# Prompt tokens in the order of their residue modulo 4, and 64 x 64 score blocks for the dilated heads of a decoder layer

## The chip, the cores and the metric

The kernel runs on one core of a Trainium2 chip. The metric is the device time of one execution in microseconds (us). Five engines take part: TensorE (PE: matmuls, and PEld: its weight loads), VectorE (DVE), ScalarE (ACT), GpSimd (POOL) and SyncE (SP, which here only issues transfers). ACT and POOL issue transfers too.

## What is computed

One layer of a hybrid decoder, for a prompt of 256 tokens and for 8 sample tokens with caches, which share all weights (D = 2048, all float32). Cut to what matters here:

```python
h = rmsnorm(x, g) * (1 + sc1) + sh1                     # modulation from c @ w_ada
q, k, v, u, ga, gb = split(h @ w_in, [1536, 3072, 4608, 5120, 7168])
for g, (window, dil) in enumerate(((128, 1), (512, 4), (2048, 16))):    # 4 heads each
    # a query reads itself and the tokens dil, 2*dil, ..., window behind it, ALiBi penalty -m_h*|t-s|
    outs[g], lses[g] = dilated_attn_prompt(q[g], k[g], v[g], dil, slopes[g])
    new_kv[g] = last min(window, T) rows of k and v
o = sum_g softmax_g(lses)[g] * outs[g]                  # 512 wide
p = pool_mixer(u)     # trailing means over 2, 4, 8, 16 tokens minus the token, 128 channels each
x = x + gt1 * ((sigmoid(ga) * (o @ w_up_attn) + sigmoid(gb) * (p @ w_up_pool)) @ w_out)
x = x + gt2 * (square(relu(h2 @ w_mlp_up)) @ w_mlp_down)
y = rmsnorm(x, g_fin)
```

Since the mixture of the three groups weighs by their softmax denominators, one softmax over all keys of the three groups gives o at once, and that is what the kernel does.

## The kernel before

Activations lie with channels on the 128 partitions and tokens along the row: 256 prompt tokens in their natural order, then the 8 sample tokens (N = 264 columns). A weight matrix streams through five `raw` tiles of 1 MB (`load`, issued by SP). ACT casts a half of such a tile to `whi` (L244), DVE takes the rest as `wlo` (L245), and PE multiplies each 128 x 128 block three times (`mm3`, L255 to L257), 264 columns each. One `whi`/`wlo` pair (three buffers) serves 24 matmuls. Beside this GEMM the modulation matrix w_ada is read as a filler (`ada_part`, L362: matmuls on 32 columns of the array each, four positions side by side, written `pa`).

The order of the instructions on each engine is made by the tile framework when the kernel is built. It interleaves the GEMM of the gates (w_in from column 5120 on), the filler and the prompt's pooling and attention, and places the waits; each engine then runs its queue strictly in that order. Transfers issued by SP and ACT take eight completion counters in turn (DMAHW0 to 7), those of POOL eight others (DMASW0 to 7). A transfer waits on its issuing queue until the one that last used its counter has landed, and what stands behind it in that queue waits with it.

The stage that the change touches:

- `pooling` (L612): four sums on DVE (L632, `up` to `a` to `b`), the means (L642 to L646) into `z`, then a matmul with w_pool (L649). The weights w_pool and the constants are loaded by POOL (L157, L606, L608), which then issues nine small stores of the sample's rows (L712). POOL clears the 16 columns ahead of the tokens (L615).
- `rows(pair, g)` (L653): for two heads of a group, PE transposes K and V (L661) into one of two PSUM buffers `px`, ACT copies them out (L666) and issues the stores to the new caches (L669). V stays, tokens on partitions, for the attention.
- `attend(slot)` (L672): for each half of the queries and the three heads of a slot, scores against all earlier keys (L679, 128 or 256 keys), the penalty and mask from `dist` (DVE, L681), one softmax (L684 to L687: a maximum on DVE, an exponential and a scaling on ACT), transposes of the weights (L692), and their product with V (L697).

The two pairs of heads follow each other: three calls of `rows`, then `attend` for two slots. The tokens of x come in at L403 and L404 and leave at L1089.

Of the kernel before, what the change touches and what calls it, by code (L numbers as in the profile page):

```python
# [30 lines left out]
T = 256  # L31
NS = 8
# [6 lines left out]
NEG = -1e30  # L39
# [16 lines left out]
def _consts():  # L56
    cols, at = [], 0

    def put(name, a):
        nonlocal at  # L60
        b = np.zeros((128, a.shape[1]), np.float32)
        b[:a.shape[0]] = a
        CONSTS[name] = (at, a.shape[1])
        cols.append(b)
        at += a.shape[1]
# [42 lines left out]
    r = i[:, None] % 32  # L108
    put("pick", np.concatenate([(r == hh * 8 + np.arange(8)[None, :]) * 1.0 for hh in range(4)], axis=1))
    marks.append(at)  # L110
    for g, dil in enumerate(DIL):
        t, s = i[:, None] + 128, np.arange(256)[None, :]
        d = t - s
        ok = (d >= 0) & (d % dil == 0) & (d <= 128 * dil)
        put(f"dist{g}", np.where(ok, -d, NEG))
    return np.concatenate(cols, axis=1).astype(np.float32), marks


# [4 lines left out]
def step_kernel(ctx, tc, x_prompt, x_sample, vectors, c_sample, kv0, kv1, kv2, state_pool, w_ada, w_in, w_up_attn,  # L123
# [472 lines left out]
    xpool.__exit__(None, None, None)  # L596
    ppool = tc.tile_pool(name="pp", bufs=1)
    ap = ppool.__enter__()
    dist = ap.tile([128, 3, 256], F32, name="dist")
    wp = ap.tile([128, 4, 128], F32, name="wpool")  # L600
    srow = ga_flat[:120, 416:928]
    mark = nc.gpsimd.tensor_copy(dummy, qkv[:, 0, 0:1])
    with tc.issue_after(mark.ins):
        nc.gpsimd.dma_start(srow, state_pool[0].rearrange("b j c -> (b j) c"))
        con_load(1, ap, nc.gpsimd)
        nc.gpsimd.dma_start(wp, w_pool.rearrange("g c d -> c g d"))  # L606
        a = CONSTS["dist0"][0]
        nc.gpsimd.dma_start(dist, consts[:, a:a + 768].rearrange("p (g c) -> p g c", g=3))  # L608


    def pooling():
        a = ga_flat[:, 2016:3104].rearrange("p (g t) -> p g t", g=4)  # L612
        b = ga_flat[:, 928:2016].rearrange("p (g t) -> p g t", g=4)
        for t in (up, a, b):
            nc.gpsimd.memset(t[:, :, :16], 0.0)  # L615
        us = up[:, :, 16 + T:]
        pr = px([15, 512])
        for g in range(4):
            nc.tensor.transpose(pr[:, g * 128:(g + 1) * 128], up[:, g, 16 + T - 15:16 + T], ident)
        prs = ap.tile([128, 768], F32, name="pt")[:15, :512]  # L620
# [5 lines left out]
        prs = ap.tile([128, 768], F32, name="sc")[:NS, :512]  # L626
        nc.scalar.copy(prs, pr)
        nc.gpsimd.dma_start(nps[0, :, 14], prs)
        src, dst = up, a
# [9 lines left out]
        nc.vector.tensor_add(z[:, :, T:], us, pw)  # L639
        for g, w in enumerate(WIN):  # L640
# [3 lines left out]
            nc.vector.scalar_tensor_tensor(z[:, g, 16:T], win[:, g, 32:], 1.0 / w, up[:, g, 32:16 + T], op0=OP.mult,  # L644
                                           op1=OP.subtract)
        nc.vector.tensor_sub(z[:, :, :16], t16, up[:, :, 16:32])  # L646
        for g in range(4):
            ps = px([128, N])
            nc.tensor.matmul(ps, wp[:, g], z[:, g], start=True, stop=True)  # L649
            nc.scalar.activation(z[:, g], ps, AF.Copy, scale=p_scale[:, g:g + 1])  # L650


    def rows(pair, g):  # L653
        hd = 4 * g + 2 * pair
        for kv in range(2):
            t0 = 1 if g == 0 and kv == 0 else 0
            src = qkv[:, 12 * (1 + kv) + hd:12 * (1 + kv) + hd + 2]
            p = px([128, 2, 256])
            for t in range(t0, 2):
                for j in range(2):  # L660
                    nc.tensor.transpose(p[:, j, t * 128:(t + 1) * 128], src[:, j, t * 128:(t + 1) * 128], ident)  # L661
            if kv:
                dst = src[:, :, :T]
            else:
                dst = ap.tile([128, 2, 256], F32, name="krow", bufs=3)
            nc.scalar.copy(dst[:, :, t0 * 128:], p[:, :, t0 * 128:])  # L666
            for t in range(1 if g == 0 else 0, 2):
                r0 = 0 if g == 0 else t * 128
                nc.scalar.dma_start(nkp[g][0, 0, r0:r0 + 128, kv, 2 * pair:2 * pair + 2, :],  # L669
                                    dst[:, :, t * 128:(t + 1) * 128])  # L670

    def attend(slot):  # L672
        for qt in range(2):
            nk = qt + 1
            sc = ap.tile([128, 3, 256], F32, name="sc")[:, :, :nk * 128]
            for g in range(3):
                hd = 4 * g + slot
                p = px([128, nk * 128])
                nc.tensor.matmul(p, qkv[:, hd, qt * 128:(qt + 1) * 128], qkv[:, 12 + hd, :nk * 128],  # L679
                                 start=True, stop=True)  # L680
                nc.vector.scalar_tensor_tensor(sc[:, g], dist[:, g, 256 - nk * 128:], SLOPES[hd], p,  # L681
                                               op0=OP.mult, op1=OP.add)
            m = ap.tile([128, 4], F32, name="m", bufs=2)
            nc.vector.tensor_reduce(m[:, 0:1], sc, axis=AX.XY, op=OP.max, negate=True)  # L684
# [3 lines left out]
            pt = ap.tile([128, 3, 2, 128], F32, name="pt")  # L688
            for kb in range(nk):
                p = px([128, 3, 128])  # L690
                for g in range(3):
                    nc.tensor.transpose(p[:, g], sc[:, g, kb * 128:(kb + 1) * 128], ident)  # L692
                nc.vector.tensor_copy(pt[:, :, kb], p)
            po = px([128, 128])
            for kb in range(nk):
                for g in range(3):
                    nc.tensor.matmul(po, qkv[:, 24 + 4 * g + slot, kb * 128:(kb + 1) * 128], pt[:, g, kb],  # L697
                                     start=kb == 0 and g == 0, stop=kb == nk - 1 and g == 2)
            nc.scalar.copy(oT[:, slot, qt * 128:(qt + 1) * 128], po)

    qd = ctx.enter_context(tc.tile_pool(name="qd", bufs=1, space=bass.MemoryType.DRAM)).tile([3, NS, 512], F32, name="qd")
    for kv in range(-1, 2):
# [9 lines left out]
            nc.gpsimd.dma_start(dst, r[32 * g:32 * g + 32])  # L712
    pooling()
    for pair in range(2):
        for g in range(3):
            rows(pair, g)
        attend(2 * pair)
        attend(2 * pair + 1)

# [412 lines left out]
```

## Time and profile before

| | |
|---|---|
| median of 3 runs (lowest to highest) | 1506.58 us (1506.47 to 1506.7) |
| the profiled execution | 1507.33 us, of which the span from first to last instruction is 1505.5 us |
| PE / PEld / DVE / ACT / POOL busy | 1478.1 / 1397.3 / 875.7 / 668.5 / 121.3 us |
| granted TensorE clock, mean | 0.997 of 2.4 GHz |
| prompt's pooling and attention | about 303 to 404 us of the span |

PE's records are pipelined, so a record's length (about 0.28 us) is longer than the distance to the next (0.12 us). Busy time of PE is therefore no proof that it does useful work all the time; the distance between the starts of records is the price of one.

### The profile page before, as it was taken

The page shows a single profiled execution, that of the slowest core. Times are in us where ns is not written, and L with a number is a line of the kernel's source. Part 1 is how long each engine was busy: PE and PEld are TensorE (multiplying, and loading weights), DVE is VectorE, ACT ScalarE, POOL GpSimd, SP SyncE. Part 2 cuts the span into 40 slices and gives each one's busy share as a digit, 9 for nine tenths or more (in the row PEclk, how much of TensorE's full clock was granted, in tenths as well). Part 3 has the DMA queues.
Part 4 walks back from the last instruction along what each step waited for, and adds up shares of the span by engine and source line. Part 5 has one row for each costly group of instructions (what it writes and reads, how often), then busy time and mean ns, then how long its engine had stood idle before and what let it go on. Part 6 is the DMA issues. An engine that isn't in the chain of part 4 may idle for free.

```text
span 1505.5 us, 29355 instructions
## 1 busy us (share of the span) xinstructions
PE 1478.1 (98%) x12454; PEld 1397.3 (93%) x12454; DVE 875.7 (58%) x1404; ACT 668.5 (44%) x992; POOL 121.3 (8%) x175
## 2 busy tenths in 40 slices
PE   7999999999999999999999999999999999999997
PEld 6899999967899889899999999999999999999997
DVE  6876656544465437765855345545555555555765
ACT  5544424334444544454645444344343444434355
POOL 0444100020101001300000000000010000100000
PEclk9999999999999999999999999999999999999998
DMA  9988987887797778677765775767576685767541
GB/s 324 326 305 283 339 297 264 331 267 262 275 318 255 260 287 319 246 261 269 242 222 208 252 235 189 252 211 246 169 265 224 213 291 175 271 231 247 203 141 58
DMA packets 162931, 377.62 MB, mean 251 GB/s; under 512 B 7233, under 2 KB 33361, under 8 KB 153192
## 3 DMA queue, kind: packets, MB, share of 16 engines
q1 hardware_dynamic: 153152, 340.02, 65.5%
q0 software_dynamic: 4064, 33.03, 6.0%
q10 hardware_dynamic: 5584, 2.69, 0.6%
q8 instruction: 98, 1.61, 0.5%
q14 instruction: 33, 0.27, 0.0%
HBM read 370.74 MB, written 26.15 MB: 264 GB/s over the span
## 4 chain that ended last, share of the span: by engine, by line
PE 89%; DMA 3%; DVE 3%; ACT 2%; issue 1%; POOL 0%; SPq 0%; ACTq 0%; DVEq 0%; POOLq 0%
PE mm L255 27%; PE mm L256 27%; PE mm L257 27%; PE pa L362 4%; DMA raw<-in_w_in_dram 2%; PE pa L310 1%; DVE wlo L245 1%; ACT whi L244 1%; DMA out_dram<-qkv 1%; DMA raw<-in_w_ada_dram 1%; PE px L697 1%; PE px L679 0%; DMA wpool<-in_w_pool_dram 0%; DVE h2lo L989 0%; POOL gate_b L913 0%
## 5 line engine op out<-in xcount | busy, mean ns | idle before, releaser
L245 DVE TENSOR_TENSOR wlo<-raw,whi 128x1024 fp32r<-128x1024 f32 x448 | 554.2, 1238 | 456.7 <-ACT whi L244 453.0
L244 ACT CAST whi<-raw 128x1024 fp32r<-128x1024 f32 x448 | 469.6, 1049 | 619.3 <-PE mm L256 581.8
L255 PE MATMUL mm<-hhi,whi 128*128 128x264 f32 x1152 | 329.8, 288 | 3.2 <-ACT whi L244 2.2
L256 PE MATMUL mm<-hlo,whi 128*128 128x264 f32 x1152 | 328.1, 286 | 0.6 <-DVE hlo L250 0.5
L257 PE MATMUL mm<-hhi,wlo 128*128 128x264 f32 x1152 | 325.3, 284 | 0.3 <-DVE wlo L245 0.2
L257 PE MATMUL mm<-ffhi,wlo 128*128 128x264 f32 x1024 | 291.9, 285 | 0.0
L255 PE MATMUL mm<-h2hi,whi 128*128 128x264 f32 (+1 forms) x1024 | 291.9, 285 | 0.0
L257 PE MATMUL mm<-h2hi,wlo 128*128 128x264 f32 (+1 forms) x1024 | 291.3, 285 | 0.5 <-DVE wlo L245 0.5
L256 PE MATMUL mm<-h2lo,whi 128*128 128x264 f32 (+1 forms) x1024 | 291.7, 285 | 0.0
L256 PE MATMUL mm<-fflo,whi 128*128 128x264 f32 x1024 | 291.5, 285 | 0.0
L255 PE MATMUL mm<-ffhi,whi 128*128 128x264 f32 x1024 | 291.4, 285 | 0.0
L255 PEld LDWEIGHTS mm<-hhi,whi 128*128 128x128 f32 x1152 | 216.5, 188 | 16.4 <-issue 9.6
L256 PEld LDWEIGHTS mm<-hlo,whi 128*128 128x128 f32 x1152 | 216.8, 188 | 1.4 <-DVE hlo L250 1.2
L257 PEld LDWEIGHTS mm<-hhi,wlo 128*128 128x128 f32 x1152 | 215.6, 188 | 1.2 <-DVE wlo L245 0.7
L255 PEld LDWEIGHTS mm<-h2hi,whi 128*128 128x128 f32 x1024 | 193.2, 189 | 2.5 <-issue 1.7
L255 PEld LDWEIGHTS mm<-ffhi,whi 128*128 128x128 f32 x1024 | 193.5, 189 | 1.7 <-issue 1.7
L256 PEld LDWEIGHTS mm<-fflo,whi 128*128 128x128 f32 x1024 | 193.5, 189 | 0.0
L257 PEld LDWEIGHTS mm<-h2hi,wlo 128*128 128x128 f32 x1024 | 192.6, 188 | 0.7 <-DVE wlo L245 0.7
L256 PEld LDWEIGHTS mm<-h2lo,whi 128*128 128x128 f32 x1024 | 192.7, 188 | 0.0
L257 PEld LDWEIGHTS mm<-ffhi,wlo 128*128 128x128 f32 x1024 | 192.4, 188 | 0.0
L255 PE MATMUL mm<-mhi,whi 128*128 128x264 f32 x256 | 73.5, 287 | 0.0
L256 PE MATMUL mm<-mlo,whi 128*128 128x264 f32 x256 | 72.8, 284 | 0.0
(279 smaller groups left out, 1385.1 us busy)
## 6 DMA issues: line engine op xcount, KB each, us to landing
raw<-in_w_in_dram SPq DMA_DIRECT2D x71, 1024.0 KB, 7.2
raw<-in_w_ada_dram SPq DMA_DIRECT2D x64, 1024.0 KB, 6.6
raw<-in_w_mlp_up_dram SPq DMA_DIRECT2D x64, 1024.0 KB, 5.6
raw<-in_w_mlp_down_dram SPq DMA_DIRECT2D x64, 1024.0 KB, 5.1
raw<-in_w_ada_dram SPq DMA_DIRECT2D x64, 512.0 KB, 8.8
raw<-in_w_out_dram SPq DMA_DIRECT2D x16, 1024.0 KB, 6.9
cv<-in_cache_kv_w_dram POOLq DMA_DIRECT2D x5, 1024.0 KB, 8.0
raw<-in_w_up_pool_dram SPq DMA_DIRECT2D x4, 1024.0 KB, 8.0
```

The source lines that it names most:

```text
L244: nc.scalar.copy(hi, v)
L245: splits.append(nc.vector.tensor_sub(lo, v, hi.bitcast(F32)))
L255: nc.tensor.matmul(ps, wh, x[0][:, kt, :n], start=start, stop=False)
L256: nc.tensor.matmul(ps, wh, x[1][:, kt, :n], start=False, stop=False)
L257: nc.tensor.matmul(ps, wl, x[0][:, kt, :n], start=False, stop=stop)
L310: i = nc.tensor.matmul(pa[32 * g:32 * g + 32, :cols], cT[:, kt], src, start=done[g] == 1, stop=done[g] == each, tile_position=(0, 32 * g))
L362: i = nc.tensor.matmul(pa[32 * g:32 * g + 32], cT[:, kt], v[:, 0, g * 512:(g + 1) * 512], start=done[0] == 1, stop=done[0] == KT, tile_pos ...
L697: nc.tensor.matmul(po, qkv[:, 24 + 4 * g + slot, kb * 128:(kb + 1) * 128], pt[:, g, kb], start=kb == 0 and g == 0, stop=kb == nk - 1 and g ...
```

## The change

Prompt tokens are laid out by residue: column c holds token 4*(c % 64) + c // 64, so that the 64 tokens of a residue modulo 4 are neighbours. The reads of x, the stores of K, V and y undo the order (`by_residue`). A query of dilation 4 can only see tokens of its own residue, one of dilation 16 a part of them, so that their scores are 64 x 64 blocks (each on half of the array's columns, `tile_position`), and the softmax of a query half runs over 384 columns of weights instead of 384 (first half) and 768 (second half). A score row for dilation 1 now always has 256 keys. V of dilations 4 and 16 is laid with its two groups on the two halves of the partitions (`vrows`), K and V of a pair are turned in one call of `rows`, and the stores of a pair are 20 instead of 10, smaller ones. Pooling works on a copy `un` of the channels in natural order.

```diff
+    at_ = np.arange(T)
+    tok = 4 * (at_ % 64) + at_ // 64
     for g, dil in enumerate(DIL):
-        t, s = i[:, None] + 128, np.arange(256)[None, :]
-        d = t - s
+        for tile_ in range(2 if g == 0 else 1):
+            q = tok[128 * tile_:128 * tile_ + 128]
+            if g == 0:
+                d = q[:, None] - tok[None, :]
+            else:
+                d = 4 * (i[:, None] % 64 - np.arange(64)[None, :])
...
+    def by_residue(rows):
+        return rows.rearrange("(u t i) d -> t i u d", t=2, i=2)
...
-    nc.sync.dma_start(xr[:, 0], x_prompt[0, :128])
-    nc.sync.dma_start(xr[:, 1], x_prompt[0, 128:])
+    xp = by_residue(x_prompt[0])
+    nc.sync.dma_start(xr[:, 0], xp[0])
+    nc.sync.dma_start(xr[:, 1], xp[1])
...
     def pooling():
...
+        nc.gpsimd.tensor_copy(us, up[:, :, 16 + T:])
+        nc.vector.tensor_copy(un[:, :, 16:].rearrange("p g (u r) -> p g r u", r=4),
+                              up[:, :, 16:16 + T].rearrange("p g (r u) -> p g r u", r=4))
-        for t in (up, a, b):
+        for t in (un, a, b):
             nc.gpsimd.memset(t[:, :, :16], 0.0)
...
-    def rows(pair, g):
+    def rows(pair):
+        def late_half(kv, t, src):
+            for i in range(2):
+                nc.scalar.dma_start(out(0, kv)[t, i], src[64 * i + 32:64 * i + 64])
+        for g in range(3):
...
+            nc.scalar.copy(dst, p)
+            for t in range(2):
+                if g:
+                    nc.scalar.dma_start(out(g, 0)[t], dst[:, t])
+                else:
+                    late_half(0, t, dst[:, t].rearrange("p (j c) -> p j c", j=2))
...
+        for g in range(2):
+            for i in range(2):
+                dst = vrows[64 * g:64 * g + 64, heads, i, :T].rearrange("p s (t c) -> p s t c", t=2)
+                (nc.scalar.copy if g else nc.vector.tensor_copy)(dst, turned[g][64 * i:64 * i + 64])
+        for t in range(2):
+            for i in range(2):
+                for g in range(2):
+                    nc.scalar.dma_start(out(1 + g, 1)[t, i],
+                                        vrows[64 * g:64 * g + 64, heads, i, t * 128:(t + 1) * 128])
...
     def attend(slot):
         for qt in range(2):
...
+            p = px([128, 384])
+            nc.tensor.matmul(p[:, :256], qkv[:, slot, cols], qkv[:, 12 + slot, :T], start=True, stop=True)
+            for g in (1, 2):
                 hd = 4 * g + slot
+                for i in range(2):
+                    c = slice((2 * qt + i) * 64, (2 * qt + i) * 64 + 64)
+                    nc.tensor.matmul(p[64 * i:64 * i + 64, 192 + 64 * g:256 + 64 * g], qkv[:, hd, c],
+                                     qkv[:, 12 + hd, c], start=True, stop=True, tile_position=(0, 64 * i))
...
+            for j in range(2):
+                nc.tensor.matmul(po, qkv[:, 24 + slot, j * 128:(j + 1) * 128], pt[:, j], start=j == 0, stop=False)
+            for i in range(2):
+                c = slice(64 * i, 64 * i + 64)
+                nc.tensor.matmul(po[:, c], vrows[:, slot, i, cols], pt[:, 2, c], start=False, stop=i == 1)
...
     for pair in range(2):
-        for g in range(3):
-            rows(pair, g)
+        rows(pair)
...
-            nc.sync.dma_start(y_prompt[0, t * 128:(t + 1) * 128, c:c + w], v)
+            nc.sync.dma_start(by_residue(y_prompt[0])[t, :, :, c:c + w], v)
```

The order that the framework makes changes only in this stage. Three places of it matter below.

**ACT's queue, the end of the first pair's K and V.** A row is line, operation, output<-input and shape; `whi` is the cast for the GEMM, `out_dram` a store, `sc` the softmax. Before:

```order
L666 COPY qkv<-px 128x2x256 [waits PE_49]
L244 CAST whi<-raw 128x1024 [waits DMAHW7_49]
L669 DMA out_dram<-qkv 128x2x128 [waits DMAHW0_49,Activation_49]
L669 DMA out_dram<-qkv 128x2x128 [waits DMAHW1_49]
L685 ACT_TABLE_LOAD [waits DMASW7_49]
L685 ACTIVATE sc,m<-sc,m 128x3x128 [waits DVE_49]
L244 CAST whi<-raw 128x1024 [waits PE_49]
```

Now:

```order
L726 DMA out_dram<-qkv 64x2x128 [waits DMAHW5_49,DVE_49]
L726 DMA out_dram<-qkv 64x2x128 [waits DMAHW7_49,Activation_49]
L726 DMA out_dram<-qkv 64x2x128 [waits DMAHW0_49,DVE_49]
L726 DMA out_dram<-qkv 64x2x128 [waits DMAHW1_49,Activation_49]
L726 DMA out_dram<-qkv 64x2x128 [waits DMAHW2_49]
L726 DMA out_dram<-qkv 64x2x128 [waits DMAHW3_49]
L726 DMA out_dram<-qkv 64x2x128 [waits DMAHW4_49]
L726 DMA out_dram<-qkv 64x2x128 [waits DMAHW6_49]
L747 ACT_TABLE_LOAD
L747 ACTIVATE sc,m<-sc,m 128x384 [waits DVE_49]
L255 CAST whi<-raw 128x1024
```

The 20 stores of a pair now stand without a `whi` cast between them (before, one stood in the middle). Counter 6 is missing among the first seven: the framework gave it to a load by SP in between, of the w_in tile after next, and the last store waits for that load to land. The load itself waits for one of the five `raw` tiles, until PE has read the fourth block of four `pa` matmuls (the middle of the run of eight shown next).

**PE's queue, the first scores of the first slot.** `px<-qkv` is a score, `pa` the filler, `mm` the GEMM. Before:

```order
L679 MATMUL px<-qkv 128x128
L362 MATMUL pa<-raw,cT 32x512
L679 MATMUL px<-qkv 128x128
L362 MATMUL pa<-raw,cT 32x512 x4
L679 MATMUL px<-qkv 128x128
L362 MATMUL pa<-raw,cT 32x512 x3
```

Now:

```order
L734 MATMUL px<-qkv 128x256
L739 MATMUL px<-qkv 64x64 x4
L268 MATMUL mm<-hhi,wlo 128x264
L266 MATMUL mm<-hhi,whi 128x264
L267 MATMUL mm<-hlo,whi 128x264
L268 MATMUL mm<-hhi,wlo 128x264
L373 MATMUL pa<-raw,cT 32x512 x8
```

The scores of a query half now stand together, and the filler's matmuls, four of which share the array, are no longer separated by them.

**POOL's queue, pooling.** Before:

```order
L615 MEMSET gate_a 128x4x16 x2
L602 COPY dummy<-qkv 128x1
L604 DMA gate_a<-in_state_pool_dram 120x512
L593 COPY qkvs<-qkv 128x288
L157 DMA cst_3837<-in_consts_dram 128x96
L606 DMA wpool<-in_w_pool_dram 128x4x128
L608 DMA dist<-in_consts_dram 128x768
L712 DMA qd<-rows 4x8x128 x3
L712 DMA out_dram<-rows 4x8x128 x6
L622 DMA out_dram<-pt 15x512
```

Now:

```order
L618 DMA wpool<-in_w_pool_dram 128x4x128
L620 DMA dist<-in_consts_dram 128x640
L774 DMA qd<-rows 4x8x128 x3
L774 DMA out_dram<-rows 4x8x128 x6
L632 MEMSET gate_a 128x4x16
L638 DMA out_dram<-krow 15x512
```

The clearing of `b`, which DVE's third sum reads, moved behind the nine small stores, because `b` now lies where `up` was until it is copied.

## Rows read from the trace of the kernel before

**Rows 1.** Page, part 1: busy us, share of the span, instructions.

```profile
PE 1478.1 (98%) x12454; PEld 1397.3 (93%) x12454; DVE 875.7 (58%) x1404; ACT 668.5 (44%) x992; POOL 121.3 (8%) x175
```

**Rows 2.** Busy time by stretch: length, each engine, granted clock, DMA share, GB/s.

```profile
320.00:404.00 84.00, 82.97 (x598) 62.76 (x598) 38.34 (x70) 34.27 (x59) 0.00 (x0) 1.00 0.81 277
404.00:470.00 66.00, 66.00 (x546) 66.00 (x545) 36.02 (x30) 27.65 (x35) 10.70 (x19) 1.00 0.87 298
```

**Rows 3.** Groups by shape, PE, 300 to 410 us: busy, mean ns, idle before.

```profile
L697 PE MATMUL px<-pt,qkv 128*128 128x128 f32 x72 | 10.0, 284 | 0.0
L679 PE MATMUL px<-qkv 128*128 128x256 f32 x24 | 7.4, 401 | 0.0
L661 PE MATMUL px<-cst,qkv 128*128 128x128 f32 x44 | 6.2, 275 | 0.0
L692 PE MATMUL px<-cst,sc 128*128 128x128 f32 x36 | 5.5, 279 | 1.0 <-ACT sc L687 1.0
L679 PE MATMUL px<-qkv 128*128 128x128 f32 x24 | 5.0, 304 | 0.0
```

**Rows 4.** The chain of waits from 300 to 404 us: start, us, what.

```profile
304.77 6.69 DMA wpool<-in_w_pool_dram
...
316.92 0.87 PE px L661 x8
...
342.69 1.45 PE px L697 x12
...
345.55 1.85 PE pa L362 x16
```

**Rows 5.** The chain of waits of the whole span, one piece.

```profile
121.33 3.67 PE pa L310 x128
```

**Rows 6.** Timeline of PE: start, us, instruction, count, idle before it.

```profile
308.33 1.03 PE L636 MATMUL px<-cst,gate_a 120*128 120x8 f32 x8 [1.34 <-DMA cst<-in_consts_dram]
...
319.97 1.04 PE L362 MATMUL pa<-raw,cT 128*32 128x512 f32 x2
...
323.76 0.39 PE L255 MATMUL mm<-hhi,whi 128*128 128x264 f32 x1
...
376.63 1.22 PE L679 MATMUL px<-qkv 128*128 128x256 f32 x4
377.49 0.47 PE L255 MATMUL mm<-hhi,whi 128*128 128x264 f32 x1
```

**Rows 7.** Timeline of POOL: the last three of the nine small stores.

```profile
312.10 1.75 POOL L712 DMA_DIRECT2D out_dram<-rows  x3 [2.45 <-DMA wpool<-in_w_pool_dram]
```

**Rows 8.** Timeline of DVE in pooling: third sum, fourth sum, a mean.

```profile
305.89 0.69 DVE L632 TENSOR_TENSOR gate_a<-gate_a 128x512 f32<-128x512 f32 x1
...
308.45 0.42 DVE L632 TENSOR_TENSOR gate_a<-gate_a 128x256 f32<-128x256 f32 x1
...
310.30 0.40 DVE L644 SCALAR_TENSOR_TENSOR z<-gate_a 128x240 f32<-128x240 f32 x1
```

**Rows 9.** Timeline of ACT and its queue (ACTq: the issue of a transfer).

```profile
315.02 0.42 ACTq L669 DMA_DIRECT2D out_dram<-krow  x1
...
320.02 1.51 ACTq L669 DMA_DIRECT2D out_dram<-krow  x2
321.57 0.59 ACT L666 COPY qkv<-px 128x512 f32<-128x512 f32 x1 [2.56 <-PE px L679]
...
324.80 1.28 ACT L685 ACT_TABLE_LOAD   x1
...
326.89 1.05 ACT L244 CAST whi<-raw 128x1024 fp32r<-128x1024 f32 x1
```

**Rows 10.** Transfers: issuing queue, count, KB each, median us to landing (three stretches).

```profile
out_dram<-krow ACTq DMA_DIRECT2D x1, 128.0 KB, 1.9
out_dram<-qkv ACTq DMA_DIRECT2D x2, 128.0 KB, 8.6
raw<-in_w_in_dram SPq DMA_DIRECT2D x12, 1024.0 KB, 5.3
```

More of the change, by code (lines that the diff above doesn't have):

```diff
@@ L598, in step_kernel @@
     ap = ppool.__enter__()
-    dist = ap.tile([128, 3, 256], F32, name="dist")
+    dist = ap.tile([128, 640], F32, name="dist")
     wp = ap.tile([128, 4, 128], F32, name="wpool")
@@ L625, in pooling @@
             nc.tensor.transpose(pr[:, g * 128:(g + 1) * 128], us[:, g], ident)
-        prs = ap.tile([128, 768], F32, name="sc")[:NS, :512]
+        prs = ap.tile([128, 2, 256], F32, name="krow", bufs=3).rearrange("p a b -> p (a b)")[:NS]
         nc.scalar.copy(prs, pr)
         nc.gpsimd.dma_start(nps[0, :, 14], prs)
-        src, dst = up, a
+        src, dst = un, a
         for lv in range(4):
@@ L639, in pooling, with quads @@
         nc.vector.tensor_add(z[:, :, T:], us, pw)
+        by = z[:, :, :T].rearrange("p g (r u) -> p g u r", r=4)
+        def quads(v):
+            return v.rearrange("p (u r) -> p u r", r=4)
         for g, w in enumerate(WIN):
@@ L650, in pooling, with out @@
             nc.scalar.activation(z[:, g], ps, AF.Copy, scale=p_scale[:, g:g + 1])
-    def rows(pair, g):
[L654 to L657, printed above, removed]
+    vcols = qkv[:, 28:36].rearrange("p (g s) n -> p g s n", g=2)
+    vrows = qkv[:, 28:36].rearrange("p (i s) n -> p s i n", i=2)
+    def rows(pair):
+        heads = slice(2 * pair, 2 * pair + 2)
+        def out(g, kv):
+            return by_residue(nkp[g][0, 0, :, kv, heads, :].rearrange("n h d -> n (h d)"))
+        def late_half(kv, t, src):
+            for i in range(2):
+                nc.scalar.dma_start(out(0, kv)[t, i], src[64 * i + 32:64 * i + 64])
+        for g in range(3):
+            src = qkv[:, 12 + 4 * g + 2 * pair:14 + 4 * g + 2 * pair, :T]
+            dst = ap.tile([128, 2, 256], F32, name="krow", bufs=3)
@@ L658, in rows @@
             p = px([128, 2, 256])
-            for t in range(t0, 2):
+            for t in range(2):
                 for j in range(2):
[L661 to L670, printed above, removed]
+                    nc.tensor.transpose(p[:, t, j * 128:(j + 1) * 128], src[:, j, t * 128:(t + 1) * 128], ident)
@@ new lines, in rows @@
+            nc.scalar.copy(dst, p)
[4 more added lines that the diff above has]
+                    late_half(0, t, dst[:, t].rearrange("p (j c) -> p j c", j=2))
+        src = qkv[:, 24 + 2 * pair:26 + 2 * pair, :T]
+        p = px([128, 2, 256])
+        for t in range(2):
+            for j in range(2):
+                nc.tensor.transpose(p[:, j, t * 128:(t + 1) * 128], src[:, j, t * 128:(t + 1) * 128], ident)
@@ new lines, in rows @@
+        nc.scalar.copy(src, p)
+        for t in range(2):
+            late_half(1, t, src[:, :, t * 128:(t + 1) * 128])
+        turned = []
+        for g in range(2):
+            p = px([128, 512]).rearrange("p (s t c) -> p s t c", s=2, t=2)
+            for t in range(2):
+                for j in range(2):
+                    nc.tensor.transpose(p[:, j, t], vcols[:, g, 2 * pair + j, t * 128:(t + 1) * 128], ident)
+            turned.append(p)
+        for g in range(2):
+            for i in range(2):
+                dst = vrows[64 * g:64 * g + 64, heads, i, :T].rearrange("p s (t c) -> p s t c", t=2)
+                (nc.scalar.copy if g else nc.vector.tensor_copy)(dst, turned[g][64 * i:64 * i + 64])
@@ L672, in attend @@
+        for t in range(2):
+            for i in range(2):
+                for g in range(2):
+                    nc.scalar.dma_start(out(1 + g, 1)[t, i],
+                                        vrows[64 * g:64 * g + 64, heads, i, t * 128:(t + 1) * 128])
     def attend(slot):
         for qt in range(2):
-            nk = qt + 1
-            sc = ap.tile([128, 3, 256], F32, name="sc")[:, :, :nk * 128]
-            for g in range(3):
-                hd = 4 * g + slot
[L678 to L681, printed above, removed]
+            cols = slice(qt * 128, qt * 128 + 128)
+            sc = ap.tile([128, 384], F32, name="sc", bufs=2)
+            p = px([128, 384])
+            nc.tensor.matmul(p[:, :256], qkv[:, slot, cols], qkv[:, 12 + slot, :T], start=True, stop=True)
+            for g in (1, 2):
+                hd = 4 * g + slot
+                for i in range(2):
+                    c = slice((2 * qt + i) * 64, (2 * qt + i) * 64 + 64)
+                    nc.tensor.matmul(p[64 * i:64 * i + 64, 192 + 64 * g:256 + 64 * g], qkv[:, hd, c],
+                                     qkv[:, 12 + hd, c], start=True, stop=True, tile_position=(0, 64 * i))
+            for g, c, b in ((0, 0, 256 * qt), (1, 256, 512), (2, 320, 576)):
+                w = 64 if g else 256
+                nc.vector.scalar_tensor_tensor(sc[:, c:c + w], dist[:, b:b + w], SLOPES[4 * g + slot], p[:, c:c + w],
@@ L682, in attend @@
                                                op0=OP.mult, op1=OP.add)
             m = ap.tile([128, 4], F32, name="m", bufs=2)
[L684 removed]
+            nc.vector.tensor_reduce(m[:, 0:1], sc, axis=AX.X, op=OP.max, negate=True)
             nc.scalar.activation(sc, sc, AF.Exp, bias=m[:, 0:1], accum_out=m[:, 1:2])
@@ L687, in attend @@
             nc.scalar.activation(sc, sc, AF.Copy, scale=m[:, 2:3])
[L688 to L693, printed above, removed]
-            po = px([128, 128])
[L695 to L699, printed above, removed]
+            pt = ap.tile([128, 3, 128], F32, name="pt", bufs=2)
+            p = px([128, 3, 128])
+            for j in range(3):
+                nc.tensor.transpose(p[:, j], sc[:, j * 128:(j + 1) * 128], ident)
+            nc.vector.tensor_copy(pt, p)
+            po = px([128, 128])
+            for j in range(2):
+                nc.tensor.matmul(po, qkv[:, 24 + slot, j * 128:(j + 1) * 128], pt[:, j], start=j == 0, stop=False)
+            for i in range(2):
+                c = slice(64 * i, 64 * i + 64)
+                nc.tensor.matmul(po[:, c], vrows[:, slot, i, cols], pt[:, 2, c], start=False, stop=i == 1)
+            nc.scalar.copy(oT[:, slot, cols], po)
     qd = ctx.enter_context(tc.tile_pool(name="qd", bufs=1, space=bass.MemoryType.DRAM)).tile([3, NS, 512], F32, name="qd")
@@ L714, in step_kernel @@
     for pair in range(2):
-        for g in range(3):
-            rows(pair, g)
+        rows(pair)
         attend(2 * pair)
```

24 lines of the change are left out of this document (13 added, 11 removed).

## The prediction

> **What bounds the kernel now.** First the shares of busy time: PE is at work for 98% of the span, the next engine for 58% [rows 1]. Then the windows: in the stage of the change (320 to 404 us) PE stands idle for 84.00 - 82.97 = 1.03 us in all, and in the 66 us behind it not at all: 546 records, 0.121 us each [rows 2]. So work that leaves PE in this stage is time won, a wait that PE meets is time lost, and no later slack takes either up: the difference made here stays to the end. The forecast is a ledger of PE's time between 304 and 404 us.
>
> A record's length overlaps its neighbours [rows 3], so prices are distances between starts. The chain of waits gives them for runs of one kind: a transpose 0.87/8 = 0.109 us, a 128-column record 1.45/12 = 0.121, a filler record 1.85/16 = 0.116 [rows 4]. A 256-column score takes (377.49 - 376.63)/4 = 0.215 per record [rows 6]. The groups show two records per float32 product and one per transpose: 72, 24, 44, 36 and 24 of them [rows 3].
>
> **The change, part by part.** Signs: plus is slower.
>
> *1. Attention's records on PE.* Before: 24 x 0.121 + 24 x 0.215 (scores) + 36 x 0.109 + 72 x 0.121 + 44 x 0.109 = 25.5 us. After: 16 scores of 256 keys, 3.4; 64 records of 64 x 64 scores; 24 transposes of weights, 2.6; 32 records of V times 128 columns, 3.9, and 32 times 64; 48 transposes of K and V, 5.2. No row shows a 64 x 64 block. Bounds: 3.67/128 = 0.0287 us, the records of 32-column filler early in the span [rows 5], and 0.11 us, the short 120 x 8 transposes one after the other (1.03/8 = 0.13 with its last record's length, 0.11 between starts) [rows 6]. I take 0.055: two blocks sit side by side on the columns, half as many as the filler's four. That is 3.5. V times 64 columns I take at the transposes' 0.11, 3.5 (bounds 0.06, half a 128-column record, and 0.121). Sum 22.2, so **-3.3** (-6.6 to +0.6).
>
> *2. The filler is no longer cut.* From the second filler matmul at 319.97 to the next GEMM record at 323.76, PE needs 3.79 us for a group of fours with scores between [rows 6]; four score records at 0.121 take 0.48 of that, and the same 16 filler records in one piece take 1.85 [rows 4]. Cutting costs 1.46 us. Three fours were cut in three so; one is still (by the softmax's transposes). **-2.9** (-4.4 to -1.5).
>
> *3. Pooling.* POOL now clears `b` behind its small stores; the last three of these end at 312.10 + 1.75 = 313.85 [rows 7], and the whole queue waits for the 6.69 us transfer of w_pool [rows 4]. From there DVE needs 0.15 for the clearing, the third and fourth sums, 0.69 + 0.42, two means at 0.40 [rows 8], and about 0.5 of small ones: 316.4. PE comes to `z` at 308.33 + 1.03 [rows 6] + 41 x 0.121 + 10 x 0.116 = 315.5. Some of that wait stands today; **+0.6** (-0.4 to +2.5, the upper end with the copy `un` not hidden). The copy, about 1.2 us by the 1024-column cast on ACT [rows 9], lies on DVE before POOL's stores are done; without that cover it is the upper end.
>
> *4. The first pair's stores.* These 20 stand in ACT's queue with no `whi` cast among them. An issue takes 0.42 us alone, 0.76 in a pair [rows 9]; 20 at 0.42 and six copies of 0.59 [rows 9] are 12 us from about 320, so 332. The last store also waits for the load that took its counter. That load waits for the `raw` tile until PE has read its fourth filler block: 316.4 + 1.6 (z times w_pool) + 6 x 0.116 + 48 x 0.121 + 24 x 0.109 + 0.7 (scores) + 8 x 0.116, some 1.8 more for switches and copies, gives 330.6. It lands 5.3 later [rows 10], 335.9. Then 0.42, the table load with the exponential, 326.89 - 324.80 = 2.09, and the cast, 1.05 [rows 9]: `whi` is ready at 339.4. PE has cover until 316.4 + 1.6 + 38 x 0.116 + 24 x 0.109 + 72 x 0.121 + 0.9 (scores) + 1.7 (switches, copies) = 336.3. It waits **3.1** (0 to 6: a load landing in 2.5 less, or in 8.6 as the stores do today [rows 10]).
>
> *5. The second pair's stores.* Again 20, and two of them wait for counters that loads of w_ada by SP hold. PE has 54 GEMM records and 21 filler matmuls, 54 x 0.121 + 42 x 0.116 = 11.4 us, to cover 20 x 0.42 + 6 x 0.59 = 11.9 and the wait for a landing, part of which runs beside it. I take **1.0** (0 to 6). The idle time PE has there today, 1.03 [rows 2], goes: the stores of before end in waits too. Parts 4 and 5 together: **+3.1**.
>
> *6. Small ones.* Eight visits to 64-column blocks at 0.1 us each, and copies out of the two `px` buffers that PE waits for (a copy is 0.59 [rows 9]): **+1.5** (0 to +3). The softmax runs over 384 columns always, and its fillers on PE last 3.4 to 4.7 us; no wait counted.
>
> *At nothing.* Moved with the rest: x and y keep the same bytes in pieces of the same length, only further apart, hidden behind PE in the stages where they lie; the new caches' stores carry the same bytes in twice the pieces, off PE's path but for parts 4 and 5. A 128 KB store with nothing beside it lands in 1.9 us today [rows 10]; if strides made it slower the cost is inside the upper ends of 4 and 5. POOL's and SP's other loads move with their queues; what they feed is used some 10 us later.
>
> Sum: -3.3 - 2.9 + 0.6 + 3.1 + 1.5 = **-1.0 us**. The profiled execution took 1507.33, so 1506.3; it lies 0.75 above the median of the runs, so the median should be **1505.6**. What a measurement can tell from no change is 0.2%, 3.0 us; the forecast lies inside that.
>
> **The rivals.**
>
> *A: the stores hold ACT far longer, slower.* Every store or load takes a counter in turn, so one late landing holds all that is queued behind it: exponential, `whi`, then PE. If the load lands in 8.6 us (as ACT's stores do in the stage [rows 10]) instead of 5.3, PE waits 6.4 in part 4, and by the same 8.6 about 5.7 in part 5: -3.3 - 2.9 + 0.6 + 12.1 - 1.0 + 1.5 = +7.0, **1513.6**. It decides from where ACT frees `whi` after 336.3. For it: DMA is 0.81 busy there, 277 GB/s [rows 2], and ACT's copy already stood idle 2.56 us in this place [rows 9]. Against: ACT is busy for 34.27 of the 84 us only [rows 2].
>
> *B: the stores are covered, faster.* The load lands early enough or the framework's counter is free by then, and PE never waits for `whi`: -3.3 - 2.9 + 0.6 - 1.0 + 1.5 = -5.1, **1501.5**. For it: PE waited only 1.03 us for all reasons in this stage [rows 2]. Against: the row of ACT's queue, which ends in that counter.
>
> *C: each visit to the 64-column blocks empties the array, slower.* The cut fours show what an interruption can cost: 1.46 us for two, 0.73 each. Eight visits at 0.73 are 5.8 instead of 0.8: -1.0 + 5.0 = +4.0, **1510.6**. It decides from 0.6 us a visit (-1.0 + 8 x 0.5 = +3.0). Against: some of the 1.46 may be fours that no longer share the array. The Trainium skill, "TensorEngine Tiling (Array Packing)", Key Properties, says that changing the tiling mode drains TensorE, which speaks for C; [rows 6] show the cost of a cut, but not that it is a drain.
>
> That the change does not do what it says: were the 64 x 64 blocks run one at a time at 0.11, part 1 loses 3.5, +2.5 in all, 1509.1; this is inside the forecast's range.
>
> **How the numbers follow.** Forecast 0.50, with its own range 1502.5 to 1509.5 (parts 2, 4 and 5 up to half-way to their ends, not all at once); A 0.20, B 0.18, C 0.12. The range, 1501.0 to 1514.0, reaches to B and past A's number; it leaves out the upper third of A and the lower third of B, and the far ends of parts 1 and 5, under 2 in 10. Faster by over 0.2%: B and a sixth of the forecast, 0.26. Slower: A, most of C and little of the forecast, 0.31. Between: 0.43.
>
> **What would show it.** 64 x 64 scores 0.055 us apart; filler fours in one piece at 1.85; PE before `z` waiting some 1 us for DVE; on ACT the last store before the table load waiting for a landing until about 336, and PE idle about 3 us at its next `whi`, 1 in the second pair. PE's idle time above 8 us between 320 and 404 would mean A, none B. Wrong altogether if PE's records are not closer in the GEMM after 404 us, or if the time changes outside the stage: at the reads of x or the last stores of y.

## The result, and the profile after

The changed kernel takes **1602.18 us** (1600.72 to 1605.16, 4 runs) beside 1506.53 us (1504.93 to 1506.7) of the kernel before on the same chip: ratio 1.064, 95% interval 1.0622 to 1.0658. The forecast was 1505.6 and the range ended at 1514.0. It is wrong by some 97 us.

Its profiled execution took 1602.35 us, span 1600.5. The shares of busy time say first that PE has no more work than before: the busy time is the same within 1.3 us [rows 1], only its share fell from 98% to 92%. The span is 95.0 us longer, so nearly all of that is waiting.

```profile
PE 1479.4 (92%) x12470; PEld 1398.6 (87%) x12470; DVE 872.9 (55%) x1405; ACT 667.0 (42%) x992; POOL 120.6 (8%) x176
```

Where it lies is read from landmarks: the same pieces of PE's work, in the same order, in both chains of waits (start, length, piece). First the kernel before: the first transposes of x that the chain names, the last filler before the stage, the sample's attention behind it, the last scaling of the residual.

```profile
12.67 1.90 PE px L456 x8
...
287.39 3.57 PE pa L362 x32
...
523.20 3.55 PE px L858 x26
...
1496.60 2.37 ACT fflo L1086 x3
```

The changed kernel:

```profile
49.19 1.90 PE px L468 x8
...
324.94 3.57 PE pa L373 x32
...
581.73 3.55 PE px L919 x26
...
1555.34 2.37 ACT fflo L1147 x3
```

The distances are 36.5, 37.6, 58.5 and 58.7 us. Behind the last landmark the span of the kernel before ends 8.9 us later (1505.5 - 1496.60), that of the changed kernel 45.2 us later (1600.5 - 1555.34). So: **+36.5 us before the transposes of x, +21.0 us in the stage of the change, +36.3 us behind the last residual, and 1.2 us elsewhere.** The forecast had looked at the second of these alone.

The start, in PE's timeline (the bracket is the idle time before and who ended it), and the queue of SP:

```profile
26.00 2.99 PE L468 MATMUL px<-cst,qkv 128*128 128x128 f32 x12 [17.98 <-DMA qkv<-in_x_prompt_dram]
48.58 0.61 PE L321 MATMUL pa<-raw,cT 128*32 128x128 f32 x2 [19.59 <-DMA raw<-in_w_ada_dram]
```

```profile
2.13 0.71 SPq L415 DMA_DIRECT2D qkv<-in_x_prompt_dram  x1
2.89 0.54 SPq L416 DMA_DIRECT2D qkv<-in_x_prompt_dram  x1
3.47 44.67 SPq L330 DMA_DIRECT2D raw<-in_w_ada_dram  x4
```

PE waits 17.98 us for the first half of x, then 19.59 for w_ada. Its first four loads stand behind x in SP's queue and take 44.67 us to be issued, and the first of them, on which PE waits, lands 44.98 us after its issue began, as the chain of waits has it:

```profile
3.47 44.98 DMA raw<-in_w_ada_dram
```

A load reports its landing in the trace by sixteen marks. Of this one, fourteen come by 25.2 us and the last two at 48.4, behind x; each load of x leaves two marks in all. The end, windows behind the last matmul (length, each engine's busy time and count, granted clock, share of the 16 DMA engines, GB/s):

```profile
1566.00:1576.00 10.00, 0.00 (x0) 0.00 (x0) 0.00 (x0) 0.00 (x0) 0.00 (x0) 0.50 0.13 51
1576.00:1596.00 20.00, 0.00 (x0) 0.00 (x0) 0.00 (x0) 0.00 (x0) 0.00 (x0) 0.50 0.13 53
```

Nothing runs but the stores of y, and these keep 0.13 of the DMA engines busy: two of sixteen, 51 GB/s, 25 GB/s each. (A share of 0.13 could also be sixteen engines at work now and then. The packets in the trace decide it: from 1570 to 1590 us two are under way at once for 19.0 of the 20 us.) When x is read in the kernel before, all sixteen are busy and move 368 to 414 GB/s, 23 to 26 each:

```profile
4.00:6.00 2.00, 0.45 (x2) 0.36 (x2) 1.75 (x5) 1.22 (x4) 0.00 (x0) 1.00 0.94 368
6.00:8.00 2.00, 1.97 (x7) 1.16 (x7) 1.14 (x6) 0.39 (x1) 0.48 (x2) 1.00 0.99 414
```

An engine is as fast as ever; there are only two of them.

In the stage, the chain of waits of the changed kernel names stores of K, and the queue of ACT behind them; PE's timeline shows who pays:

```profile
364.35 13.41 DMA out_dram<-krow
...
418.67 6.00 ACTq L701
424.71 11.01 DMA out_dram<-krow
```

```profile
385.26 0.59 PE L266 MATMUL mm<-hhi,whi 128*128 128x264 f32 x1 [10.73 <-ACT whi L255]
...
441.84 0.59 PE L266 MATMUL mm<-hhi,whi 128*128 128x264 f32 x1 [12.26 <-ACT whi L255]
```

PE waits 10.73 and 12.26 us for `whi`, once per pair of heads: ACT stands in its stores. This is the wait of the forecast's parts 4 and 5, several times as long.

### The profile page after: what moved, and what is told of

Same layout as the page of the kernel before. It is cut to its first block, busy times and chain, and to the rows that moved or that the text cites. A ratio compares the mean times of both kernels' runs of the same rounds, so it can differ in the third digit from the quotient of the medians.

```text
span 1600.5 us, 29404 instructions
## 1 busy us (share of the span) xinstructions
PE 1479.4 (92%) x12470; PEld 1398.6 (87%) x12470; DVE 872.9 (55%) x1405; ACT 667.0 (42%) x992; POOL 120.6 (8%) x176
## 4 chain that ended last, share of the span: by engine, by line
PE 85%; DMA 5%; DVE 3%; ACT 2%; ACTq 1%; issue 1%; POOL 0%; SPq 0%; POOLq 0%
PE mm L266 26%; PE mm L267 26%; PE mm L268 26%; PE pa L373 3%; DMA raw<-in_w_ada_dram 3%; PE pa L321 2%; DMA out_dram<-krow 2%; DVE wlo L256 1%; ACT whi L255 1%; ACTq L726 1%; ACTq L701 0%; DVE h2lo L1050 0%; POOL gate_b L974 0%; PE px L1105 0%; PE px L757 0%
## 5 line engine op out<-in xcount | busy, mean ns | idle before, releaser
L266 PE MATMUL mm<-hhi,whi 128*128 128x264 f32 x1152 | 330.8, 289 | 26.2 <-ACT whi L255 25.2
```

Of the source, the lines that this page charges most:

```text
L266: nc.tensor.matmul(ps, wh, x[0][:, kt, :n], start=start, stop=False)
```

## The experiments

**Two theories of the slow transfers.** What x, y and the K stores of dilations 4 and 16 have in common is the pattern `t i u d` of `by_residue`, of which a transfer takes one `t`: it counts two (`i`) outermost, then 64 rows four apart. *Two engines*: the count of two outermost confines the transfer to two DMA engines. *Distance*: rows four apart are slow. First the reads of x alone, cut so that `i` is no longer inside a transfer, the rows as far apart as before:

```diff
-    nc.sync.dma_start(xr[:, 0], xp[0])
-    nc.sync.dma_start(xr[:, 1], xp[1])
+    for t in range(2):
+        for i in range(2):
+            nc.sync.dma_start(xr[64 * i:64 * i + 64, t], xp[t, i])
```

> The reads of x alone are cut in two by residue, 64 rows each, same rows, same distance between rows. Theory 'two engines' (a transfer whose pattern in memory counts two in its outermost place is carried by two of the 16 DMA engines: 2 MB moved at about 50 GB/s with the DMA share at 0.12 to 0.17 in the first 45 us): x lands before 15 us instead of 47, the start is as before, 36.5 us less, about 1565.7 us. Rival 'distance' (rows four apart are slow to read): two more issues and nothing else changes, about 1602 us. If a part of both holds, between them.

Measured: 1568.71 us, ratio to the kernel before 1.0413 (1.0383 to 1.0443), 33.5 us less than the changed kernel. Then the counter-test, the two outermost kept, the rows made neighbours:

```diff
-    xp = by_residue(x_prompt[0])
+    xp = x_prompt[0].rearrange("(i t u) d -> t i u d", t=2, i=2)
```

> The reads of x still count two in the outermost place, but the rows inside are neighbours (the tokens of x then stand in another order than the rest of the kernel assumes, so the output's tokens are computed in another order). 'Two engines': as slow as the changed kernel, 1602 us (1598 to 1606). 'Distance': the start is as before, about 1566 us.

Measured: 1601.32 us, ratio 1.063 (1.0599 to 1.066): as slow as the changed kernel (the tokens are in another order here, so only the time counts). Distance is out, twice: rows far apart are fast without the two, neighbouring rows are slow with it. The stores of y, cut likewise:

```diff
-            nc.sync.dma_start(by_residue(y_prompt[0])[t, :, :, c:c + w], v)
+            for i in range(2):
+                nc.sync.dma_start(by_residue(y_prompt[0])[t, i, :, c:c + w], v[64 * i:64 * i + 64])
```

> The stores of y alone are cut in two by residue. 'Two engines': the tail behind PE's last matmul shrinks from about 43 us to about 7, so 36 us less, about 1566 us; 'distance': still about 1602 us.

Measured: 1569.57 us, ratio 1.0419 (1.0377 to 1.046), 32.6 us less. And the K stores:

```diff
-                    nc.scalar.dma_start(out(g, 0)[t], dst[:, t])
+                    for i in range(2):
+                        nc.scalar.dma_start(out(g, 0)[t, i], dst[64 * i:64 * i + 64, t])
```

> The stores of K of dilations 4 and 16 alone are cut in two, 24 instead of 20 stores per pair of heads. Between start and tail the changed kernel loses 21 to 22 us. 'Two engines': the stores of K (13.4 and 11.0 us in the chain of waits) hold ACT's queue, and nearly all of the 21 us goes: about 1580 us (1578 to 1586). Rival 'burst' (the number of stores and the counters they take hold ACT, as rival A of the prediction): at most half goes or it gets longer with more stores: 1590 us or more.

Measured: 1590.06 us, ratio 1.0555 (1.0524 to 1.0585), 12.1 us less. The time lies at the edge of what 'burst' expected, but more than half of the 21 us went, which 'burst' did not allow: each theory has a part. Two engines are 12 of the stage's 21 us; 9 stay. In PE's waits of this run between 350 and 450 us (total, times, longest) the wait for `whi` is still there, and the windows behind its first half show a second price, the granted clock:

```profile
PE mm L266 <- ACT whi L255: 10.6, 2, 6.3
```

```profile
376.00:378.00 2.00, 0.00 (x0) 0.00 (x0) 0.00 (x0) 0.00 (x0) 0.00 (x0) 1.00 0.95 301
...
380.00:382.00 2.00, 0.71 (x3) 0.71 (x4) 0.90 (x2) 1.98 (x5) 0.00 (x0) 0.50 0.98 406
382.00:384.00 2.00, 2.00 (x11) 2.00 (x11) 1.28 (x3) 2.00 (x3) 0.00 (x0) 0.50 1.03 386
...
386.00:388.00 2.00, 2.00 (x20) 1.60 (x19) 1.08 (x5) 0.27 (x1) 0.00 (x0) 1.00 1.02 393
```

```profile
381.68 0.42 PE L267 MATMUL mm<-hlo,whi 128*128 128x264 f32 x1
381.90 0.42 PE L266 MATMUL mm<-hhi,whi 128*128 128x264 f32 x1
...
387.04 0.28 PE L267 MATMUL mm<-hlo,whi 128*128 128x264 f32 x1
387.16 0.28 PE L268 MATMUL mm<-hhi,wlo 128*128 128x264 f32 x1
```

PE idles 6.28 us, its clock is granted at 0.50 (1.2 GHz) when it starts again, and it gets through 11 records in 2 us where it makes 20, of another mix, at 1.00 (2.4 GHz); GEMM records alone start 0.22 us apart there and 0.12 at 1.00. The three cuts together:

> Reads of x, stores of y and stores of K of dilations 4 and 16 are all cut in two by residue, so that no transfer counts two in its outermost place. If the three costs are independent: 1602.2 - 33.5 - 32.6 - 12.1 = 1524 us (1521 to 1527). If one of them hid another: more than 1530 or less than 1518.

Measured: 1523.43 us, ratio 1.0113 (1.0099 to 1.0126). The sum of the three, 1524, is met, so the costs are independent. That leaves 17 us over the kernel before.

**What is left at the start and the end.** With x cut by residue the first transposes still come late, at 225 GB/s though all engines are busy (first row; length, engines, clock, share, GB/s). The kernel before with nothing changed but its x and y in transfers of 64 rows, natural order:

```diff
-    nc.sync.dma_start(xr[:, 0], x_prompt[0, :128])
-    nc.sync.dma_start(xr[:, 1], x_prompt[0, 128:])
+    for t in range(2):
+        for i in range(2):
+            r = 128 * t + 64 * i
+            nc.sync.dma_start(xr[64 * i:64 * i + 64, t], x_prompt[0, r:r + 64])
...
```

> The kernel before, with its reads of x and stores of y cut into transfers of 64 neighbouring rows, nothing else. With x cut by residue the start stays 4 us late, at 225 GB/s where the kernel before has about 390. Theory 'half the partitions' (a transfer that fills 64 partitions moves at about half the rate, here two after the other): +4 us at the start and about +4 in the tail, 1514 us. Theory 'distance' (rows four apart are slow): 1506.5 to 1508 us, only the issues of six more stores and two more reads.

Measured: 1515.05 us, ratio 1.0055 (1.0039 to 1.007), 8.4 us more. Against it, whole tiles of 128 partitions, but every other row, of x and of y:

```diff
-    nc.sync.dma_start(xr[:, 0], x_prompt[0, :128])
-    nc.sync.dma_start(xr[:, 1], x_prompt[0, 128:])
+    xp = x_prompt[0].rearrange("(p t) d -> t p d", t=2)
+    nc.sync.dma_start(xr[:, 0], xp[0])
+    nc.sync.dma_start(xr[:, 1], xp[1])
...
```

> The kernel before, with every other row of x on the 128 partitions of a transfer, and of y likewise (the prompt's tokens then stand in another order than attention and pooling assume). 'Half the partitions': as the kernel before, 1506.5 us (1505 to 1508). 'Distance': +3 to +8 us, 1510 to 1514 us.

Measured: 1506.05 us, ratio 0.9997 (0.9988 to 1.0006): no cost (again the time alone counts, the tokens being in another order). The same 2 us of the start in three runs, x cut by residue, the halves, and every other row:

```profile
6.00:8.00 2.00, 1.98 (x7) 1.19 (x6) 1.13 (x5) 0.00 (x0) 0.48 (x2) 1.00 1.04 225
```

```profile
6.00:8.00 2.00, 1.90 (x6) 1.01 (x5) 1.14 (x6) 0.00 (x0) 0.48 (x2) 1.00 0.96 213
```

```profile
6.00:8.00 2.00, 1.98 (x7) 1.17 (x7) 1.14 (x6) 0.50 (x1) 0.48 (x2) 1.00 1.00 418
```

A transfer on 64 partitions moves half as much, with the DMA engines just as busy. That it is also smaller is not the reason: stores of y of 256 KB move 378 GB/s on 128 partitions (kernel before, 1498 to 1500 us) and 234 on 64 (the halves, 1506 to 1508 us). By the landmarks the halves lose 3.4 us at the start (290.77 - 287.39) and 3.9 at the end (1511.70 - 1498.95 = 12.75 beside 8.88). So some half of the 17 us is the price of this way to mend it, not of the change's idea.

**What is left in the stage.** All cuts kept, and every store of `rows` issued by POOL:

```diff
-                        nc.scalar.dma_start(out(g, 0)[t, i], dst[64 * i:64 * i + 64, t])
+                        nc.gpsimd.dma_start(out(g, 0)[t, i], dst[64 * i:64 * i + 64, t])
...
```

> As with all three cut, and the stores of K and V are issued by POOL, which has nothing to do there, instead of ACT. Theory 'burst' (rival A: ACT is held by its stores, PE waits for whi 6.3 and 4.7 us and runs at the lower clock for some 6 us behind each, worth about 3 us each): 15 to 17 us less than with the stores on ACT, about 1508 us (1505 to 1512). Rival 'landing' (loads land late beside the stores, whoever issues them): over 1518 us.

Measured: 1511.19 us, ratio 1.003 (1.0019 to 1.0041), 12.2 us less than with the stores on ACT; 15 to 17 were expected. PE's waits between 310 and 425 us are then these two:

```profile
PE px L653 <- DMA cst<-in_consts_dram: 0.6, 1, 0.6
PE px L672 <- issue: 0.3, 1, 0.3
```

The wait for `whi` is gone: it was the stores in ACT's queue that held the casts. (The stores on POOL also no longer share counters with SP's loads, so issue and counters are not told apart by this run.) Measured from the sample's first transpose to the sample's attention, the stage takes 218.55 us in the kernel before (304.65 to 523.20), 239.53 in the changed one (342.20 to 581.73), 227.72 with all cuts (307.88 to 535.60) and 214.22 here (308.00 to 522.22). So without the transfers' costs the stage is 4.3 us shorter than before.

**A version from this.** The stores stay on POOL. Since 128 partitions with every other row cost nothing, x is read and y stored so, and the order by residue is made by copies that stand there anyway (behind the transposes of x, in the broadcast of the norm's factors, in the scaling before y's transposes) and by two small ones added before the last sum of squares:

```diff
+    xp = x_prompt[0].rearrange("(p t) d -> t p d", t=2)
...
+                xT[:, d:d + 4, :T].rearrange("p k (i t u) -> p t k i u", i=2, t=2)[:, t],
+                p.rearrange("p k (u i) -> p k i u", i=2))
...
+            nc.sync.dma_start(y_prompt[0].rearrange("(p t) d -> t p d", t=2)[t, :, c:c + w], v)
...
```

> Stores of K and V on POOL as in the run before, and x and y on 128 partitions again: a transfer takes every other token, and the order by residue is made by the copies that stand behind the transposes of x, by the copy that broadcasts the norm's factors, and by the scaling of the last residual before its transposes. If 'half the partitions' is the whole rest: 1511.2 - 8.4 = 1502.8 us, within 1501 and 1505, which is 2 to 5 us under the kernel before. Rival: the strided copies at the start and the extra copies at the end cost more than 2 us: 1505 to 1508 us.

Measured: 1502.56 us, ratio 0.9971 (0.996 to 0.9983): faster than the changed kernel and the one before. Is it the blocks of scores that win, or POOL? The control, the kernel before with its stores on POOL:

```diff
-                nc.scalar.dma_start(nkp[g][0, 0, r0:r0 + 128, kv, 2 * pair:2 * pair + 2, :],
+                nc.gpsimd.dma_start(nkp[g][0, 0, r0:r0 + 128, kv, 2 * pair:2 * pair + 2, :],
```

> The kernel before with its K and V stores issued by POOL, nothing else. If the smaller blocks of scores (and not the place of the stores) give the 5 us that the run with stores on POOL won in the stage: 1505.5 to 1506.7 us, since PE waits 1.03 us in the stage of the kernel before at most. If the place of the stores gives it: about 1502 us.

Measured: 1501.47 us, ratio 0.997 (0.9957 to 0.9983). The expectation that the blocks give the gain fell: this small edit alone wins as much. Its stage takes 213.84 us (302.01 to 515.85), 4.7 less than before; PE's waits between 296 and 425 us fell by 1.3 of this (2.8 to 1.5). PE's groups by shape between 296 and 425 us (busy, mean ns) say how. The filler in the kernel before, in the control, and in the version with the blocks:

```profile
L362 PE MATMUL pa<-raw,cT 128*32 128x512 f32 x128 | 21.2, 601 | 0.0
```

```profile
L362 PE MATMUL pa<-raw,cT 128*32 128x512 f32 x128 | 16.6, 599 | 0.0
```

```profile
L373 PE MATMUL pa<-raw,cT 128*32 128x512 f32 x128 | 22.0, 601 | 0.0
```

The same 128 records, 4.6 us of busy time apart between the first two. The framework makes the order anew for each kernel, and moving the stores changes how often a score or a transpose lands inside a four. In filler matmuls, the pieces of the runs that are cut are (1 4 3) three times, (5 3) and (1 7) in the kernel before, (1 4 3) once in the control, (5 3), (5 3), (1 7), (1 4 3), (1 7), (1 4 3) in the version. What the blocks win there, the cuts take. So the second to fourth matmul of each four were given precedence, in both:

```diff
+            i = nc.tensor.matmul(pa[:32], cT[:, kt], v[:, 0, :512], start=done[0] == 1, stop=done[0] == KT,
+                                 tile_position=(0, 0))
+            with tc.issue_after(i.ins), tc.high_priority():
+                for g in range(1, 4):
...
```

> As the run with x and y on 128 partitions, and the second to fourth matmul of each four of the filler are given precedence over whatever else is ready, so that no score or transpose stands inside a four (runs of 4 and 8, where the run before has pieces of 5 3, 1 7 and 1 4 3). Theory 'cut fours': the filler's busy time in the stage, 22.0 us for 128 records, falls to about 16, and the stage is 5 to 6 us shorter: 1497 us (1495.5 to 1499). Rival: the time of a cut four is only time of the scores that stand in it, so nothing changes: 1502 to 1503 us.

Measured: 1498.7 us, ratio 0.9954 (0.994 to 0.9968), **the fastest**. It ran on another chip than the run without precedence; by the ratios to the kernel before it is 2.6 us faster, less than the 5 to 6 expected. The filler falls to 16.1 us (the line counts the second to fourth matmuls; the first ones run beside them, 16.0), but the stage shortens by 2.0 us only, from 214.75 (305.04 to 519.79) to 212.77 (304.86 to 517.63). Transposes of weights now wait for the softmax on ACT, 1.7 us, where they waited 0.4; where the rest of the filler's gain went is open, and a part of a cut four's busy time may be time of the scores that stand in it:

```profile
L376 PE MATMUL pa<-raw,cT 128*32 128x512 f32 x96 | 16.1, 601 | 0.0
...
L760 PE MATMUL px<-cst,sc 128*128 128x128 f32 x24 | 4.3, 289 | 1.7 <-ACT sc L756 1.4
```

> The kernel before with its stores of K and V on POOL and the same precedence inside a four. There the framework cuts one run alone (1 4 3) once the stores are on POOL, filler 16.6 us busy, so 'cut fours' expects 0.5 to 1.5 us less than the run before it, 1500 to 1501 us. The distance to the other run of this pair is then what the 64 x 64 blocks themselves are worth: by part 1 of the prediction, 3.3 us. If they are worth nothing: both at the same time.

Measured: 1503.97 us, ratio 0.9989 (0.998 to 0.9998), 2.9 us more than without precedence by the ratios, where 0.5 to 1.5 less was expected. The filler's 15.9 us are 0.7 less, but a new wait costs more, scores behind a copy of ACT:

```profile
L365 PE MATMUL pa<-raw,cT 128*32 128x512 f32 x96 | 15.9, 601 | 0.0
...
L682 PE MATMUL px<-qkv 128*128 128x256 f32 x24 | 8.0, 425 | 1.9 <-ACT oT L702 1.9
```

Of this pair the version with the blocks is 5 us faster; of the pair without precedence it is 1 us slower, a difference inside the intervals. The order decides both, so this does not measure the blocks alone; part 1 below does.

## Why the prediction was wrong, point by point

**The step that failed is "At nothing".** It said that x and y "keep the same bytes in pieces of the same length, only further apart, hidden behind PE in the stages where they lie", and that the cache's stores are "off PE's path but for parts 4 and 5". Same bytes, same pieces: true. But how many engines carry a transfer was not asked, and the count of two stands in the diff for all to read. And nothing hides x or y: PE has nothing to do before x lands, and behind the last residual nothing runs but y. The two ends cost 36.5 and 36.3 us, and cutting x and y took 33.5 and 32.6 of it back; the rest, 3.0 and 3.7, is about what 64 partitions cost in the run of the halves, 3.4 and 3.9. For the cache's stores the prediction did allow for slow strides, "inside the upper ends of 4 and 5", 12 us in all; the two waits came to 23.0. A row of the kernel before would have priced the step: 2 MB at two engines of 25 GB/s are some 40 us.

The Trainium skill has this, in "DMA: Bandwidth & Descriptors", under Rules for kernel authors: the slowest dimension above one of the patterns sets how many engines take part, and an outermost one smaller than 16 confines the transfer to as many at most. The trace agrees: 0.13 of 16 in the tail, and 1601.32 us with neighbouring rows. The same list wants 128 partitions, and transfers of 1 MiB or more, for the full rate; here 64 partitions moved 225 against about 400 GB/s.

**Parts 4 and 5** took the right wait and too short: 3.1 and 1.0 us, where PE waited 10.73 and 12.26. With the K stores on all engines, nothing else cut, it is 6.28 and 4.35 (10.6 in all), and the stage is +9.2 (569.81 - 342.08 = 227.73 beside 218.55). Rival A, one late landing that holds ACT's queue, said 6.4 and 5.7, and +7.0. What held the first wait in that run:

```profile
369.25 5.15 DMA raw<-in_w_in_dram
374.42 3.86 DMA out_dram<-qkv
378.30 1.28 ACT L748
```

The load that had taken the counter landed in 5.15 us, close to the forecast's 5.3 and not in A's 8.6. Behind it the last store waited for the counter of an earlier store, issued at 369.93 and landed at 377.64: that was the late landing. So A had the kind of wait right and the transfer wrong; that its 6.4 comes so close to 6.28 is in part luck. What A left out is the clock: behind the two waits 11 and 12 records in 2 us instead of 20. A's chance was put at 0.20, because ACT's busy time looked small, and busy time does not count a queue that waits. In the changed kernel itself the stores of K on two engines lengthened the same wait.

**Rival B**, no wait for `whi`, was worked out at -5.1; with the stores on POOL the stage is -4.3. The sum is right within 1 us once the transfers are out of it, but in part by luck, since part 2 was wrong and PE's waits made up for it (2.8 us between 296 and 425 before, 0.9 with the stores on POOL). Part by part:

- *Part 1*, -3.3: in the run with all cuts and the stores on POOL, attention's eight groups are 5.5 + 5.3 + 4.5 + 4.2 + 3.6 + 3.5 + 2.4 + 1.3 = 30.3 us busy, in the kernel before 34.1 [rows 3], **-3.8**. A 64 x 64 record costs 0.38/8 = 0.048 us (taken: 0.055; next start less first), one of V times 64 columns 0.40/4 = 0.10 (taken: 0.11):

```profile
374.86 0.56 PE L762 MATMUL px<-pt,qkv 128*128 128x64 f32 x4
375.26 0.65 PE L736 MATMUL px<-qkv 128*128 128x256 f32 x2
375.84 0.45 PE L741 MATMUL px<-qkv 128*64 128x64 f32 x8
376.22 1.92 PE L373 MATMUL pa<-raw,cT 128*32 128x512 f32 x14
```

- *Part 2*, -2.9: in the changed kernel the filler went from 21.2 to 19.4, -1.8, a part of it at half the clock; with POOL's stores +0.8. The price of a cut, 1.46 for two, held: five cut runs in the kernel before, three of three pieces and two of two, come to 3 x 1.46 + 2 x 0.73 = 5.8, and 21.2 less 16.6 with one such run is 4.6 (5.8 - 1.46 = 4.4). What failed is to take it for a gain of the change: it is one of the order, which moved here with an edit as small as the place of the stores. The prediction also counted three cut runs before and one after; before there were five.
- *Part 3*, +0.6: PE waited 0.4 us ahead of `z` in the changed kernel, 0.5 before; nothing.
- *Part 6*, +1.5, was about right: eight visits at the price below are 1.2, and in the changed kernel PE waited 0.8 for one copy out of `px`.
- *Rival C*: the two records of a 256-key score ahead of the small blocks take 0.58 (375.26 to 375.84) instead of 2 x 0.215, so a visit costs some 0.15 us, not 0.73; all eight visits of this run lie between 0.58 and 0.63. Rival C fell; whether the 0.15 us is a drain, no run shows.

What the prediction named as the sign that it is wrong altogether, time changed "at the reads of x or the last stores of y", is what came.

## What to carry to other kernels

When a layout is permuted, price each transfer by its new pattern: read off the outermost count and the partitions, and divide the bytes by that many engines' rate. A transfer that feeds the first instruction or drains the last one is on the path whatever the busy shares say. And before a gain of a few microseconds is put down to an edit, look whether the framework's order moved with it: the control with one small edit won as much here.

## What the runs showed that was not expected

- A store or load whose pattern counts two outermost: 0.13 of the DMA engines, 51 GB/s, some 40 us for 2 MB; the first load behind it in the same queue landed after 44.98 us, its last two of sixteen parts 23 us behind the others.
- Reads of x on 64 partitions: 213 to 225 GB/s with the DMA engines 0.96 to 1.04 busy, against 414 and 418 on 128. Row distance: no cost (1506.05 us with every other row).
- Groups of scores or transposes that stand inside the filler's fours cost as much as the blocks save in attention: with eight such places instead of two the same 128 filler records are busy 4.6 us longer; attention's groups save 3.8.
- With the K stores cut, PE stood idle for 6.28 and 4.35 us, and both times it came back at a granted clock of 0.50: GEMM records 0.22 us apart instead of 0.12.
